# Modulation steps of four tied products, and weights listed in one order and split two k-tiles ahead, in a two-block fp32 network on one core

## The chip, the cores and the metric

The kernel runs on one core of one Trainium2 chip. The metric is the device time of that core in microseconds. TensorE is called PE, VectorE DVE, ScalarE ACT, GpSimd POOL and SyncE SP; SP issues most of the DMAs here, in order.

## The reference

Two blocks in fp32, on 256 tokens of width 2048 with 256 tokens of context. The first block has two layers; each turns a conditioning vector c (and another one for the context) into shift, scale and gate, modulates the normed tokens with them and multiplies with one wide matrix:

```python
for l in range(DEPTH):
    shift, scale, gate = jnp.split(sc @ w_ada[l] + b_ada[l], 3, axis=-1)      # sc = silu(c)
    shift_c, scale_c, gate_c = jnp.split(scc @ w_ada[l] + b_ada[l], 3, axis=-1)
    h = rms(x, norm_w[l]) * (1.0 + scale[:, None]) + shift[:, None]
    hc = rms(xc, norm_w[l]) * (1.0 + scale_c) + shift_c
    qa, ka, va, qb, kb, vb, qc, kc, vc, z = project_stream(h, *weights, rope=(cos, sin))
    ...                                                    # the same for hc, three attentions
    x = x + gate[:, None] * merge_out(o_a, o_b, o_c, z, w_out[l])
```

The second block follows with a token mixer (spatial gating and gated linear attention), a cross attention to a memory, and a convolutional feed-forward:

```python
y = token_mixer(h, w_in, ...);             x = x + rmsnorm(y, post_norm_mix)
y = memory_cross_attention(h, m, ...);     x = x + rmsnorm(y, post_norm_xa)
y = conv_ffn(h, w_up, conv_w, conv_b, w_down);  x = x + rmsnorm(y, post_norm_ffn)
```

## The kernel before

Every large product in fp32 is made of three matmuls of a rounded type. Each operand is split into hi (the value rounded, a copy by ACT, line 376) and lo (the rest, a subtraction by DVE, line 377), and the products are hi by hi, hi by lo and lo by hi. `dense` (lines 420 to 422) has a block of 128 tokens as the stationary operand and 512 weight columns as the moving one; `denseT` (lines 440 to 443) is its transposed form. A k-tile is 128 rows of a weight. `weights` loads two k-tiles with one DMA of 512 KB into one of three tiles `raw`, and splits both into hi and lo tiles, four of each.

In the program each call of `weights` stands at its place, but the framework's scheduler puts the instructions into the order of each engine by priorities and by when buffers come free, so a split may be placed ahead of products that stand before it in the program. The order of each engine is fixed when the kernel is built, and each engine works its own queue in that order.

Stage one (`first_products`) makes the columns of w_in that need the modulation first. The 16 k-tiles of h = modulated x are taken in five parts, `PARTS` = (0,2), (2,2), (4,4), (8,4), (12,4), as first k-tile and count, and called part 0 to part 4 here. A part has three chunks of 512 columns by four blocks of 128 tokens: 72 matmuls named L0firstd in parts 0 and 1, 144 in the others. While part i is multiplied, the modulation of part i+1 is worked out by `ada_pe`: W = 128n columns of shift and W of scale, as 16 steps of one k-tile each. Such a step loads its piece of w_ada (256 KB per DMA) into tiles `raw` of a ring of five and issues two products on the tile `adao`, with the 32-column stationary operand `cstat` (silu of c) and fp32 operands (line 629). The products go to one of four 32-partition places of one PSUM bank, by the k-tile's parity and by shift or scale. After the last step ACT copies the bank (line 634), PE transposes it (line 637), DVE adds the places up, and the next k-tiles of h can be made (transposes `trs`, line 468; hi and lo of h, lines 483 and 484).

The steps are jobs that a planner issues between dense matmuls, one each `self.every` microseconds of its own count of time:

```python
self.every = n * len(chunks) * 2.56 / FIRST
```

In later stages a part of w_ada's work is done by DVE instead (line 668).

Of the kernel before, what the change touches and what calls it, by code (L numbers as in the profile page):

```python
# [10 lines left out]
F32 = mybir.dt.float32  # L11
F32R = mybir.dt.float32r
# [4 lines left out]
UNITS = 50  # L17
FIRST = 20
D = 2048
NKT = D // 128  # L20
# [120 lines left out]


class Weights:


    def __init__(self, ap, name):
        self.ap, self.at, o = ap, {}, 0
# [45 lines left out]
class K:  # L193
# [8 lines left out]
    def __init__(self, ctx, tc, a):  # L202
        self.tc, self.nc, self.a = tc, tc.nc, a
        nc = self.nc
# [8 lines left out]
        self.ps = ctx.enter_context(tc.tile_pool(name="psum", bufs=1, space=bass.MemoryType.PSUM))  # L213
        self.nu = self.alt = 0
        self.vt = self.const.tile([128, NVT], F32, name="vt")
# [173 lines left out]
    def weights(self, w, k0, pieces):  # L389

        nc = self.nc
        raw = self.str.tile([128, 2, 512], F32, name=self.name("raw"), tag="raw", bufs=3)
        n, src = w.block(k0, pieces)
        nc.sync.dma_start(raw[:, :, :n], src)
        out = []
        for j in range(2):
            hi = self.str.tile([128, 512], F32R, name=self.name("hi"), tag="hi", bufs=4)
            lo = self.str.tile([128, 512], F32R, name=self.name("lo"), tag="lo", bufs=4)
            self.split(hi[:, :n], lo[:, :n], raw[:, j, :n])
            out.append((hi, lo))  # L400
        return out

    def dense(self, act, kts, w, pieces, cols, evac, what="d", skip={}):


        nc = self.nc
        n = sum(p[1] for p in pieces)
        ps = {t: self.psum("d", what) for t in cols}
        for i in range(0, len(kts), 2):
# [3 lines left out]
            if ks[-1] == kts[-1]:  # L413
                steps.sort(key=lambda s: cols.index(s[1]))
            for kt, t in steps:
                hi, lo = wt[kt - ks[0]]
# [10 lines left out]
    def denseT(self, act, w, pieces, evac, what="e"):  # L427
# [5 lines left out]
        for k0 in range(0, nk, 2):  # L433
            for j, (hi, lo) in enumerate(self.weights(w, k0, pieces)):
                kt = k0 + j
                xh, xl = act.part(kt, 0), act.part(kt, 1)
                for c in range(nt):
# [140 lines left out]
class Block1(K):  # L578
# [27 lines left out]
    def ada_pe(self, k0, n, cst, done):  # L606
# [6 lines left out]

        def step(kt):
            if kt == 0:
                st[0] = self.psum("o", "ada")
            acc = st[0]
            at = w.offset + k0 * 128 * D * 2 + kt * 128 * 2 * W
            if 2 * W <= 512:
                raw = self.temp("raw", tag="PT", bufs=5)  # L620
                nc.sync.dma_start(raw[:, :2 * W], bass.AP(tensor=w.tensor, offset=at, ap=[[2 * W, 128], [1, 2 * W]]))
                raws = raw[:, :W], raw[:, W:2 * W]
            else:
                raws = [self.temp("raw", tag="PT", bufs=5) for _ in range(2)]
                for b in range(2):
                    nc.sync.dma_start(raws[b], bass.AP(tensor=w.tensor, offset=at + b * W, ap=[[2 * W, 128], [1, W]]))
            for b in range(2):
                q = 64 * (kt % 2) + 32 * b
                nc.tensor.matmul(acc[q:q + 32, :W], lhsT=cst[:, kt, :], rhs=raws[b], start=kt < 2,
                                 stop=kt >= NKT - 2, skip_group_check=True)  # L630

# [12 lines left out]

        return [lambda kt=kt: step(kt) for kt in range(NKT)] + [end]

# [690 lines left out]
    def block1(self):  # L1337
        nc, a, tc = self.nc, self.a, self.tc
        with ExitStack() as es:
# [591 lines left out]
```

## Time and profile before

| | |
|---|---|
| median of 3 runs | 3528.77 us (3526.76 to 3531.81) |
| profiled execution | 3528.03 us, its span 3526.3 us |
| PE busy | 3420.2 us (97%) |
| PE weight loads busy | 2952.3 us (84%) |
| DVE busy | 2299.7 us (65%) |
| ACT busy | 1785.4 us (51%) |
| POOL busy | 321.7 us (9%) |
| DMA | 590.45 MB, mean 167 GB/s |
| mean granted clock of PE | 0.983 |

Busy times are of one profiled execution. Weight loads (PEld) lie beside matmuls. Neighbouring matmuls overlap in the records, so what one costs is read from the distance between starts. A matmul with fp32 operands leaves two records, so "x2" on the tile adao is one product. A clock of 1.00 is 2.4 GHz, of 0.50 1.2 GHz.

### The profile page before, as it was taken

The page shows a single profiled execution, that of the slowest core. Times are in us where ns is not written, and L with a number is a line of the kernel's source. Part 1 is how long each engine was busy: PE and PEld are TensorE (multiplying, and loading weights), DVE is VectorE, ACT ScalarE, POOL GpSimd, SP SyncE. Part 2 cuts the span into 40 slices and gives each one's busy share as a digit, 9 for nine tenths or more (in the row PEclk, how much of TensorE's full clock was granted, in tenths as well). Part 3 has the DMA queues.
Part 4 walks back from the last instruction along what each step waited for, and adds up shares of the span by engine and source line. Part 5 has one row for each costly group of instructions (what it writes and reads, how often), then busy time and mean ns, then how long its engine had stood idle before and what let it go on. Part 6 is the DMA issues. An engine that isn't in the chain of part 4 may idle for free.

```text
span 3526.3 us, 57200 instructions
## 1 busy us (share of the span) xinstructions
PE 3420.2 (97%) x20842; PEld 2952.3 (84%) x20842; DVE 2299.7 (65%) x4939; ACT 1785.4 (51%) x3554; POOL 321.7 (9%) x472
## 2 busy tenths in 40 slices
PE   8999999999999998999999999999999899999998
PEld 3467778888787888887777999999978899999886
DVE  2359889868876475887673555555566766666554
ACT  3235556336525355766463445444555555555544
POOL 0012221103110031111110000000000000000000
PEclk9999999999999999999998999999999999999999
DMA  7745544642465434445544535555655455555555
GB/s 257 228 147 172 140 129 132 210 161 73 145 212 182 156 115 134 144 154 156 161 151 137 186 116 184 184 181 186 197 177 169 147 184 183 183 185 190 194 192 166
DMA packets 226778, 590.45 MB, mean 167 GB/s; under 512 B 39904, under 2 KB 63184, under 8 KB 226496
## 3 DMA queue, kind: packets, MB, share of 16 engines
q1 hardware_dynamic: 221104, 570.41, 50.6%
q0 software_dynamic: 4864, 15.69, 1.4%
q8 instruction: 163, 2.67, 0.3%
q14 instruction: 119, 0.97, 0.1%
q10 hardware_dynamic: 528, 0.71, 0.1%
HBM read 582.48 MB, written 4.24 MB: 166 GB/s over the span
## 4 chain that ended last, share of the span: by engine, by line
PE 54%; issue 12%; DVE 4%; ACT 1%; POOL 1%; DMA 1%; POOLq 0%; SPq 0%; DVEq 0%; ACTq 0%
PE upd L442 5%; PE upd L440 5%; PE upd L443 5%; PE downd L420 2%; PE downd L422 2%; PE downd L421 2%; PE L0outd L420 1%; PE L0outd L422 1%; PE L0outd L421 1%; PE Ss L529 1%; DVE lo L377 1%; PE oo L572 1%; PE vd L420 1%; PE vd L422 1%; PE vd L421 1%
## 5 line engine op out<-in xcount | busy, mean ns | idle before, releaser
L377 DVE TENSOR_TENSOR lo<-raw,hi 128x512 fp32r<-128x512 f32 (+3 forms) x1788 | 1204.5, 679 | 892.0 <-ACT hi L376 886.1
L376 ACT ACTIVATE hi<-raw 128x512 fp32r<-128x512 f32 (+3 forms) x1788 | 1089.7, 614 | 1299.7 <-PE upd L442 190.8
L440 PE MATMUL upd<-hi,hi 128*128 128x256 f32 x1408 | 399.2, 284 | 0.0
L442 PE MATMUL upd<-lo,hi 128*128 128x256 f32 x1408 | 399.1, 283 | 0.0
L443 PE MATMUL upd<-hi,lo 128*128 128x256 f32 x1408 | 398.8, 283 | 0.0
L668 DVE SCALAR_TENSOR_TENSOR scr<-raw,cb 128x512 f32<-128x512 f32 x448 | 297.4, 692 | 26.0 <-DMA raw<-in_w_ada_dram 13.4
L442 PEld LDWEIGHTS upd<-lo,hi 128*128 128x128 f32 x1408 | 270.8, 192 | 0.3 <-DVE lo L484 0.3
L443 PEld LDWEIGHTS upd<-hi,lo 128*128 128x128 f32 x1408 | 270.8, 192 | 0.0
L440 PEld LDWEIGHTS upd<-hi,hi 128*128 128x128 f32 x1408 | 270.7, 192 | 0.0
L355 POOL TENSOR_TENSOR sm<-sm,mhalf 128x2 f32<-128x2 f32 (+4 forms) x116 | 116.7, 1008 | 1401.9 <-DVE sm L354 1396.3
L420 PE MATMUL downd<-hi,hi 128*128 128x512 f32 x352 | 137.7, 391 | 0.0
L422 PE MATMUL downd<-hi,lo 128*128 128x512 f32 x352 | 137.7, 391 | 0.0
L421 PE MATMUL downd<-lo,hi 128*128 128x512 f32 x352 | 137.6, 391 | 0.0
L540 ACT ACTIVATE P<-Ss,sm 128x512 f32<-128x512 f32 (+1 forms) x164 | 99.5, 607 | 67.7 <-DVE sm L536 45.9
L364 ACT ACTIVATE PT<-pTt 128x256 f32<-128x256 f32 x226 | 79.1, 380 | 63.6 <-PE pTt L557 56.2
L420 PE MATMUL L0outd<-hi,hi 128*128 128x512 f32 x256 | 101.2, 395 | 4.3 <-DVE ot L1290 3.0
L443 PE MATMUL L0zd<-hi,lo 128*128 128x512 f32 x256 | 99.7, 392 | 0.9 <-DVE lo L377 0.9
L440 PE MATMUL L0zd<-hi,hi 128*128 128x512 f32 x256 | 100.3, 392 | 0.0
L536 DVE TENSOR_REDUCE sm<-Ss 128x1 f32<-128x512 f32 (+1 forms) x164 | 95.6, 586 | 7.2 <-PE Ss L529 6.3
L442 PE MATMUL L0zd<-lo,hi 128*128 128x512 f32 x256 | 100.1, 391 | 0.0
L421 PE MATMUL L0outd<-lo,hi 128*128 128x512 f32 x256 | 100.1, 391 | 0.0
L422 PE MATMUL L0outd<-hi,lo 128*128 128x512 f32 x256 | 99.3, 391 | 0.2 <-DVE lo L377 0.2
(568 smaller groups left out, 9006.2 us busy)
## 6 DMA issues: line engine op xcount, KB each, us to landing
raw<-in_w_in_dram SPq DMA_DIRECT2D x344, 512.0 KB, 3.5
raw<-in_w_ada_dram SPq DMA_DIRECT2D x384, 256.0 KB, 3.1
raw<-in_ffn_w_up_dram SPq DMA_DIRECT2D x176, 512.0 KB, 3.5
raw<-in_w_out_dram SPq DMA_DIRECT2D x104, 512.0 KB, 4.2
raw<-in_ffn_w_down_dram SPq DMA_DIRECT2D x88, 512.0 KB, 3.9
raw<-in_w_proj_b_dram SPq DMA_DIRECT2D x32, 512.0 KB, 3.7
raw<-in_w_in_dram SPq DMA_DIRECT2D x32, 288.0 KB, 3.3
raw<-in_w_proj_a_dram SPq DMA_DIRECT2D x16, 512.0 KB, 4.3
```

Source lines behind the costliest of these rows:

```text
L355: nc.gpsimd.tensor_tensor(r, ms, self.mhalf[:, :n], op=OP.pow)
L376: self.nc.scalar.activation(hi, src, AF.Copy)
L377: self.nc.vector.tensor_sub(lo, src, hi.bitcast(F32))
L420: nc.tensor.matmul(ps[t][:, a], lhsT=xh, rhs=hi[:, a], start=first, stop=False)
L421: nc.tensor.matmul(ps[t][:, a], lhsT=xh, rhs=lo[:, a], start=False, stop=False)
L422: nc.tensor.matmul(ps[t][:, a], lhsT=xl, rhs=hi[:, a], start=False, stop=last)
L440: nc.tensor.matmul(p, lhsT=hi[:, s], rhs=xh, start=kt == 0 and c % per == 0, stop=False, skip_group_check=True)
L442: nc.tensor.matmul(p, lhsT=hi[:, s], rhs=xl, start=False, stop=False, skip_group_check=True)
L443: nc.tensor.matmul(p, lhsT=lo[:, s], rhs=xh, start=False, stop=kt == nk - 1, skip_group_check=True)
L536: nc.vector.tensor_reduce(nm[:, 0:1], S[:, :nk], op=OP.max, axis=AX.X, negate=True)
L540: nc.scalar.activation(P[:, :nk], S[:, :nk], AF.Exp, bias=nm[:, 0:1], accum_out=nm[:, 1:2])
L668: nc.vector.scalar_tensor_tensor(self.temp("scr"), raw, 1.0, st[s], op0=OP.mult, op1=OP.mult, accum_out=st["p"][:, s, k, q:q + 1])
```

## The change

A step of `ada_pe` now covers two k-tiles and issues four products, one for each of the four places, in the reverse of the order of their loads; the first three of these are tied in TensorE's order to the instruction traced before them (`keep_in_program_order`). The ring has eight tiles in place of five (the three more are taken from another tag). A part has 8 steps and an end in place of 16 and an end, and `FIRST` goes from 20 to 11. At the start a step is issued after every second load of x. The second half of the change is a list of all weights in the order of their use, `order()`. `weights` takes finished splits from a queue `whole`; `run_ahead` loads and splits the next k-tile of the list while the queue holds fewer than two, whatever product it belongs to. It is called twice in each pair of k-tiles of `dense`, and once a k-tile in `denseT`. The numbers of raw, hi and lo buffers stay the same.

```diff
-FIRST = 20
+FIRST = 11
...
+def order():
+    out = []
+    def use(name, pieces, k0=0, n=None):
+        out.extend((name, k, pieces) for k in range(k0, k0 + (n or CHUNKS[name][0] // 128), 2))
...
     def weights(self, w, k0, pieces):
-        nc = self.nc
-        raw = self.str.tile([128, 2, 512], F32, name=self.name("raw"), tag="raw", bufs=3)
-        n, src = w.block(k0, pieces)
-        nc.sync.dma_start(raw[:, :, :n], src)
-        out = []
-        for j in range(2):
-            hi = self.str.tile([128, 512], F32R, name=self.name("hi"), tag="hi", bufs=4)
-            lo = self.str.tile([128, 512], F32R, name=self.name("lo"), tag="lo", bufs=4)
-            self.split(hi[:, :n], lo[:, :n], raw[:, j, :n])
-            out.append((hi, lo))
-        return out
+        assert self.order[self.taken] == (w.name, k0, pieces), (self.order[self.taken], w.name, k0, pieces)
+        self.taken += 1
+        while len(self.whole) < 2:
+            self.run_ahead()
+        return [self.whole.pop(0) for _ in range(2)]
+
+    def load(self):
+        if self.order_at < len(self.order):
+            name, k0, pieces = self.order[self.order_at]
+            self.order_at += 1
+            raw = self.str.tile([128, 2, 512], F32, name=self.name("raw"), tag="raw", bufs=3)
+            n, src = self.w(name).block(k0, pieces)
+            self.nc.sync.dma_start(raw[:, :, :n], src)
+            self.loaded += [raw[:, j, :n] for j in range(2)]
+
+    def run_ahead(self):
+        if not self.loaded:
+            self.load()
+        if self.loaded and len(self.whole) < 2:
+            raw = self.loaded.pop(0)
+            n = raw.shape[-1]
+            hi, lo = (self.str.tile([128, 512], F32R, name=self.name(x), tag=x, bufs=4) for x in ("hi", "lo"))
+            self.split(hi[:, :n], lo[:, :n], raw)
+            self.whole.append((hi, lo))
...
-            for kt, t in steps:
+            for s, (kt, t) in enumerate(steps):
+                if s % -(-len(steps) // 2) == 0:
+                    self.run_ahead()
...
                 kt = k0 + j
+                self.run_ahead()
...
-        def step(kt):
-            if kt == 0:
+        def tile():
+            self.ada_at = (self.ada_at + 1) % 8
+            return self.temp("raw", tag="P", bufs=3) if 4 <= self.ada_at < 7 else self.temp("raw", tag="PT", bufs=5)
+
+        def step(kt0):
+            if kt0 == 0:
                 st[0] = self.psum("o", "ada")
             acc = st[0]
...
-            for b in range(2):
+            for kt, b in reversed(raws):
                 q = 64 * (kt % 2) + 32 * b
-                nc.tensor.matmul(acc[q:q + 32, :W], lhsT=cst[:, kt, :], rhs=raws[b], start=kt < 2,
-                                 stop=kt >= NKT - 2, skip_group_check=True)
+                m = nc.tensor.matmul(acc[q:q + 32, :W], lhsT=cst[:, kt, :], rhs=raws[kt, b], start=kt < 2,
+                                     stop=kt >= NKT - 2, skip_group_check=True)
+                if (kt, b) != (kt0 + 1, 1):
+                    self.tc.keep_in_program_order(m)
...
-        return [lambda kt=kt: step(kt) for kt in range(NKT)] + [end]
+        return [lambda kt=kt: step(kt) for kt in range(0, NKT, 2)] + [end]
...
                 nc.sync.dma_start(x, src)
-                first[i]()
+                if i % 2:
+                    first[i // 2]()
```

Lines move with the change: 629 becomes 698, 420 to 422 become 481 to 483, 376 and 377 become 420 and 421, 668 becomes 739, 902 becomes 973, and 729 and 732 become 800 and 803.

How the order of instructions changes is seen at two places. The first is on PE in stage one, where part 1 is multiplied and part 2's modulation is worked out (numbers behind a name tell its copies apart). Before:

```order
L629 MATMUL adao_579<-raw_608,cstat_130 32x512
L420 MATMUL L0firstd_565<-hi_568,hi_524 128x512
L421 MATMUL L0firstd_565<-lo_569,hi_524 128x512
L422 MATMUL L0firstd_565<-hi_568,lo_525 128x512
L629 MATMUL adao_579<-raw_616,cstat_130 32x512
L629 MATMUL adao_579<-raw_617,cstat_130 32x512
L420 MATMUL L0firstd_565<-hi_572,hi_537 128x512
L421 MATMUL L0firstd_565<-lo_573,hi_537 128x512
L422 MATMUL L0firstd_565<-hi_572,lo_538 128x512
L420 MATMUL L0firstd_647<-hi_653,hi_524 128x512
L629 MATMUL adao_579<-raw_625,cstat_130 32x512
L421 MATMUL L0firstd_647<-lo_654,hi_524 128x512
```

With the change, at the start of the same part:

```order
L481 MATMUL L0firstd_572<-hi_494,hi_524 128x512
L482 MATMUL L0firstd_572<-lo_495,hi_524 128x512
L698 MATMUL adao_585<-raw_592,cstat_130 32x512
L698 MATMUL adao_585<-raw_590,cstat_130 32x512
L698 MATMUL adao_585<-raw_588,cstat_130 32x512
L698 MATMUL adao_585<-raw_586,cstat_130 32x512
L481 MATMUL L0firstd_573<-hi_494,hi_524 128x512
L483 MATMUL L0firstd_572<-hi_494,lo_525 128x512
L481 MATMUL L0firstd_572<-hi_546,hi_537 128x512
L698 MATMUL adao_585<-raw_604,cstat_130 32x512
L698 MATMUL adao_585<-raw_602,cstat_130 32x512
L698 MATMUL adao_585<-raw_600,cstat_130 32x512
```

The modulation's products stood alone or in pairs between dense matmuls; now four stand in a row each time. PE's order of the changed kernel has 24 such groups of W = 512 (one spot has two groups in a row) and, behind the first L0firstd, 8 of W = 256; between the transposes ahead of the first L0firstd none is left.

The second place is on DVE in the product L0cq, late in the first layer, where lo of the weight is made beside the normalizing (lines 729, 732 and 902) and the other share of the modulation (line 668). Before:

```order
L902 TENSOR_TENSOR b_1262_4935<-b_1262_4935,sm_5000 128x512
L729 TENSOR_TENSOR rt_5054<-b_1261_4933,rSqb_1870 128x384
L732 TENSOR_TENSOR ro_5053<-b_1261_4933,rCqb_1869 128x384
L729 TENSOR_TENSOR rt_5058<-b_1261_4933,rSkb_1877 128x128
L732 TENSOR_TENSOR ro_5053<-b_1261_4933,rCkb_1876 128x128
L668 SCALAR_TENSOR_TENSOR scr_5064,adaP_4975<-raw_1309_5062,cb_4976 128x512
L668 SCALAR_TENSOR_TENSOR scr_5066,adaP_4975<-raw_1309_5062,cb_4978 128x512
L668 SCALAR_TENSOR_TENSOR scr_5070,adaP_4975<-raw_1312_5068,cb_4976 128x512
L668 SCALAR_TENSOR_TENSOR scr_5072,adaP_4975<-raw_1312_5068,cb_4978 128x512
L902 TENSOR_TENSOR b_1263_4937<-b_1263_4937,sm_5011 128x512
L377 TENSOR_TENSOR lo_5097<-raw_5094,hi_5096 128x512
L377 TENSOR_TENSOR lo_5101<-raw_5094,hi_5100 128x512
```

With the change, at the same place:

```order
L421 TENSOR_TENSOR lo_5049<-raw_5046,hi_5048 128x512
L973 TENSOR_TENSOR b_1266_4943<-b_1266_4943,sm_4975 128x512
L973 TENSOR_TENSOR b_1267_4945<-b_1267_4945,sm_5006 128x512
L800 TENSOR_TENSOR rt_5060<-b_1266_4943,rSqb_1880 128x384
L803 TENSOR_TENSOR ro_5059<-b_1266_4943,rCqb_1879 128x384
L800 TENSOR_TENSOR rt_5064<-b_1266_4943,rSkb_1887 128x128
L803 TENSOR_TENSOR ro_5059<-b_1266_4943,rCkb_1886 128x128
L739 SCALAR_TENSOR_TENSOR scr_5070,adaP_4981<-raw_1312_5068,cb_4982 128x512
L739 SCALAR_TENSOR_TENSOR scr_5072,adaP_4981<-raw_1312_5068,cb_4984 128x512
L739 SCALAR_TENSOR_TENSOR scr_5076,adaP_4981<-raw_1315_5074,cb_4982 128x512
L739 SCALAR_TENSOR_TENSOR scr_5078,adaP_4981<-raw_1315_5074,cb_4984 128x512
L973 TENSOR_TENSOR b_1268_4947<-b_1268_4947,sm_5017 128x512
```

The 117th lo of the program, lo_5097 before and lo_5049 after, stood behind the four steps of line 668 and the product of line 902 and now stands ahead of them; the 118th, lo_5101 before, stands right behind the last of these rows, as it did.

## Rows read from the trace of the kernel before

**Rows 1.** The page's busy time of each engine, its share of the span, and instructions.
```profile
PE 3420.2 (97%) x20842; PEld 2952.3 (84%) x20842; DVE 2299.7 (65%) x4939; ACT 1785.4 (51%) x3554; POOL 321.7 (9%) x472
```

**Rows 2.** Timeline, PE's first dense product and ACT ahead of it: start, duration.
```profile
33.51 0.61 ACT L483 ACTIVATE hi<-h 128x512 fp32r<-128x512 f32 x1
...
36.10 0.48 PE L420 MATMUL L0firstd<-hi,hi 128*128 128x512 f32 x1
```

**Rows 3.** Stretches: length; PE, PEld, DVE, ACT, POOL busy (instructions); PE clock, DMA share, GB/s.
```profile
60.00:114.00 54.00, 52.72 (x180) 19.78 (x178) 19.01 (x41) 10.32 (x21) 0.00 (x0) 1.00 0.63 196
114.00:168.00 54.00, 54.00 (x221) 30.16 (x223) 23.14 (x43) 15.22 (x28) 0.00 (x0) 1.00 0.75 251
3350.00:3400.00 50.00, 50.00 (x220) 41.17 (x220) 26.19 (x40) 24.64 (x41) 0.00 (x0) 1.00 0.59 192
```

**Rows 4.** The same view for the instructions on the tile adao alone.
```profile
36.00:60.00 24.00, 8.22 (x54) 1.87 (x52) 0.38 (x1) 1.00 0.70 222
60.00:212.00 152.00, 60.89 (x192) 8.22 (x192) 1.80 (x3) 1.00 0.69 226
```

**Rows 5.** Timeline of PE: one product alone, four together, a pair with W = 256.
```profile
99.79 0.40 PE L422 MATMUL L0firstd<-hi,lo 128*128 128x512 f32 x1
100.12 1.04 PE L629 MATMUL adao<-raw,cstat 128*32 128x512 f32 x2
...
101.43 0.39 PE L421 MATMUL L0firstd<-lo,hi 128*128 128x512 f32 x1
...
167.52 0.39 PE L422 MATMUL L0firstd<-hi,lo 128*128 128x512 f32 x1
167.84 1.06 PE L629 MATMUL adao<-raw,cstat 128*32 128x512 f32 x8
...
169.17 0.39 PE L421 MATMUL L0firstd<-lo,hi 128*128 128x512 f32 x1
...
56.00 0.40 PE L422 MATMUL L0firstd<-hi,lo 128*128 128x512 f32 x1
56.33 0.63 PE L629 MATMUL adao<-raw,cstat 128*32 128x256 f32 x4
...
57.22 0.39 PE L421 MATMUL L0firstd<-lo,hi 128*128 128x512 f32 x1
```

**Rows 6.** Timeline of PE at the border between part 1 and part 2.
```profile
109.33 0.66 PE L637 MATMUL adat<-ident,ada 128*128 128x128 f32 x4 [0.69 <-ACT ada L634]
...
111.57 0.55 PE L468 MATMUL trs<-ident,x 128*128 128x128 f32 x3 [0.60 <-DVE h L478]
```

**Rows 7.** A stretch at the start, columns as in the third group.
```profile
20.00:30.00 10.00, 8.70 (x38) 2.52 (x35) 0.62 (x4) 5.08 (x16) 1.09 (x2) 0.50 1.05 391
```

**Rows 8.** DMA issues (median us to landing), SP's issues, and what SP waited for.
```profile
raw<-in_w_ada_dram SPq DMA_DIRECT2D x131, 256.0 KB, 3.4
...
121.09 0.81 SPq L626 DMA_DIRECT2D raw<-in_w_ada_dram  x2
...
SPq L626 <- PE adao L629: 67.0, 41, 3.9
```

**Rows 9.** What PE waited for over the whole span: us, times, longest.
```profile
PE L1qbd L420 <- ACT hi L376: 5.1, 1, 5.1
...
PE L0cqd L421 <- DVE lo L377: 3.9, 2, 3.2
```

**Rows 10.** Timeline of PE after its longest wait in L0cq, and that stretch.
```profile
529.57 0.50 PE L421 MATMUL L0cqd<-lo,hi 128*128 128x512 f32 x1 [3.16 <-DVE lo L377]
...
530.83 0.63 PE L420 MATMUL L0cqd<-hi,hi 128*128 128x512 f32 x1
531.26 0.63 PE L421 MATMUL L0cqd<-lo,hi 128*128 128x512 f32 x1
...
530.00:533.50 3.50, 3.50 (x11) 2.69 (x10) 3.50 (x11) 0.00 (x0) 0.00 (x0) 0.54 0.78 249
```

**Rows 11.** Table loads of ACT: busy time, mean ns of one.
```profile
L1493 ACT ACT_TABLE_LOAD x3 | 3.8, 1283 | 0.1
```

More of the change, by code (lines that the diff above doesn't have):

```diff
@@ L140, in packed_ada @@
     return np.concatenate(out)
+def order():
+    out = []
+    def use(name, pieces, k0=0, n=None):
+        out.extend((name, k, pieces) for k in range(k0, k0 + (n or CHUNKS[name][0] // 128), 2))
+    A = [[(256 * i, 256), (512 + 256 * i, 256)] for i in range(2)]
+    ckv = [[(3584, 288)], [(3872, 288)]]
+    for k0, n in PARTS:
+        for p in [[(1024, 512)]] + A:
+            use("w_in0", p, k0, n)
+    for p in [[(2560, 512)], [(1536, 384), (2304, 128)], _Z[0], [(1920, 384), (2432, 128)], [(3072, 512)], *ckv,
+              _Z[3], _Z[1], _Z[2]]:
+        use("w_in0", p)
+    for l in range(2):
+        if l:
+            for p in [[(2816, 256)], [(1024, 512)], *A, [(2304, 512)], *ckv, [(1536, 384)], [(1920, 384)],
+                      [(3072, 512)], _Z[3], _Z[2]]:
+                use("w_in1", p)
+        for j in range(3):
+            use(f"w_qb{l}", [(384 * j, 384)])
+            use(f"w_kvb{l}", [(512 * j, 512)])
+            if l and j < 2:
+                use("w_in1", _Z[j])
+        for j in range(4):
+            for _ in range(2 if not l and j == 3 else 1):
+                use(f"w_out{l}", [(512 * j, 512)])
+    for p in CHUNKS["w_in_2"][1][:3] + _N512(4, 4096):
+        use("w_in_2", p)
+    for c in (2048, 3072, 2560, 3584, 0, 512, *range(6144, 8192, 512)):
+        use("w_in_2", [(c, 512)])
+    for n in range(4):
+        use("w_in_2", [(8208 + 512 * n, 512)])
+        use("w_in_2", [(10256 + 512 * n, 512)])
+        use("w_proj_a_2", [(512 * n, 512)])
+        use("w_proj_b_2", [(512 * n, 512)])
+    for n in ("w_out_2", "xa_wk_2", "xa_wq_2", "xa_wv_2", "xa_wo_2", "ffn_w_up_2", "ffn_w_down_2"):
+        for p in CHUNKS[n][1]:
+            use(n, p)
+    return out
 class Weights:
     def __init__(self, ap, name):
-        self.ap, self.at, o = ap, {}, 0
+        self.name, self.ap, self.at, o = name, ap, {}, 0
         rows, chunks = CHUNKS[name]
@@ L213, in __init__ @@
         self.ps = ctx.enter_context(tc.tile_pool(name="psum", bufs=1, space=bass.MemoryType.PSUM))
-        self.nu = self.alt = 0
+        self.nu = self.alt = self.ada_at = 0
+        self.order, self.loaded, self.whole, self.taken, self.order_at = order(), [], [], 0, 0
         self.vt = self.const.tile([128, NVT], F32, name="vt")
@@ L612, in ada_pe @@
         st = {}
-        def step(kt):
-            if kt == 0:
+        def tile():
[3 more added lines that the diff above has]
+            if kt0 == 0:
                 st[0] = self.psum("o", "ada")
             acc = st[0]
[L618 to L624, printed above, removed]
+            raws = {}
+            for kt in (kt0, kt0 + 1):
+                at = w.offset + k0 * 128 * D * 2 + kt * 128 * 2 * W
+                if 2 * W <= 512:
+                    raw = tile()
+                    nc.sync.dma_start(raw[:, :2 * W], bass.AP(tensor=w.tensor, offset=at, ap=[[2 * W, 128], [1, 2 * W]]))
+                    raws[kt, 0], raws[kt, 1] = raw[:, :W], raw[:, W:2 * W]
+                    continue
                 for b in range(2):
-                    nc.sync.dma_start(raws[b], bass.AP(tensor=w.tensor, offset=at + b * W, ap=[[2 * W, 128], [1, W]]))
-            for b in range(2):
+                    raws[kt, b] = tile()
+                    nc.sync.dma_start(raws[kt, b], bass.AP(tensor=w.tensor, offset=at + b * W,
+                                                           ap=[[2 * W, 128], [1, W]]))
+            for kt, b in reversed(raws):
                 q = 64 * (kt % 2) + 32 * b
-                nc.tensor.matmul(acc[q:q + 32, :W], lhsT=cst[:, kt, :], rhs=raws[b], start=kt < 2,
-                                 stop=kt >= NKT - 2, skip_group_check=True)
+                m = nc.tensor.matmul(acc[q:q + 32, :W], lhsT=cst[:, kt, :], rhs=raws[kt, b], start=kt < 2,
+                                     stop=kt >= NKT - 2, skip_group_check=True)
+                if (kt, b) != (kt0 + 1, 1):
+                    self.tc.keep_in_program_order(m)
         def end():
```

## The prediction, made before the changed kernel ran

> **What bounds the kernel now.** The page's busy times come first: PE is busy 97% of the span [rows 1]. So a change is worth what it takes out of PE's own row, and work that goes away on another engine is worth nothing. The stretches come next, because both edits to the modulation lie in stage one, from the first L0firstd product at 36.10 us [rows 2] to the last at about 255. In the stretches 60–114 and 114–168 PE is busy 52.72 and 54.00 of 54 us, with 0.63 and 0.75 of the DMA share and a clock of 1.00 [rows 3]. PE bounds stage one, and the transfers have room. The same stretches for the tile adao alone show whose busy time that is: 60.89 of 152 us from 60 to 212 belong to the modulation's products, and 8.22 us more from 36 to 60 [rows 4]. That is the place to look, since a dense 128x512 product costs 50.00/220 = 0.227 us [rows 3].
>
> **What a stop for the modulation costs.** PE's timeline tells it by the starts, not by the durations, since matmuls overlap. A lone product (two records, x2) at 100.12 stands between a dense product at 99.79 and the second one after it at 101.43: 1.64 us, where two dense pitches would be 0.45. The one stop with four products (x8) at 167.84 takes 169.17 − 167.52 = 1.65 us [rows 5]. So a stop costs 1.64 − 0.45 = 1.19 us whether one or four products stand in it: the products of four different 32-partition places run side by side, 1.04 us for one and 1.06 for four. With W = 256 a pair at 56.33 costs 57.22 − 56.00 − 0.45 = 0.76 us [rows 5].
> Now the number of stops. 60.89 us at about 1.05 each are 58 stops of W = 512 [rows 4, 5], for 192 records, which is 96 products: 1.66 products in a stop. 8.22/0.63 = 13 stops of W = 256 lie behind the first dense product.
>
> **The change part by part.**
> *Tying.* The order of the changed kernel has every group as four in a row: 24 groups of W = 512 and 8 of W = 256 behind the first dense product; the first part's steps before 30 us stay bound by the DMA (391 GB/s, share 1.05 [rows 7]) and are costed at nothing. Stops saved: 58 − 24 = 34, times 1.19 = 40.5 us; 13 − 8 = 5, times 0.76 = 3.8 us.
> On the cost of four together the Trainium skill speaks against the row. Its page "TensorE: Matmul & The Clock Gate", section "Measured speedup vs the span model", gives three column tiles side by side a speedup of 2.38, not 3. As an estimate from that page a stop would take 1.26 times a lone one, 0.27 us more, and 24 of them would give 6.5 us back; the trace does not agree, with 1.06 for four against 1.04 for one.
> *Some stops were cover.* At the border of part one PE waits 0.69 us for ACT before the transposes at 109.33, and 0.60 for h before those at 111.57, with three of part 3's products in between that fill the rest [rows 6]. With the stops gone from there such waits are bare: four stops near 107–114 had partly cost nothing. I take 2 us off (0 to 4.8, which is 4 x 1.19).
> *Start.* Before, three W = 256 pairs stand among the transposes ahead of the first dense product at 36.10; in the new order none does. ACT's hi of h starts at 33.51 and takes 0.61 [rows 2], so the first dense product could start at about 34.2: 1.9 us (0 to 1.9). PE runs at a clock of 0.50 in 20–30 [rows 7] and is still at it when the transposes begin, and when it has less to do there that stretch may end later: 1 us against it (0 to 3.5, as long as the stretch of half clock at 530 [rows 10]).
> *Transfers of tied groups.* A group needs four tiles, and the ring has eight, so the loads for a group start when the group two before it is done. While part one's 72 dense products run, the new order has 16 to 27 of them between such groups, which with the group between is 16 x 0.227 + 1.19 = 4.8 us to 7.3 us. Needed are two issues of 0.81 us for two each, and 3.4 us to landing [rows 8]: 5.0 us. In the parts of 144 dense products it is 6 to 8 us. So the stretch of part one sits at the edge; per byte too, since 16 k-tiles of w_ada (8.4 MB) and three loads of w_in (1.6 MB) have to come in 72 x 0.227 + 8 x 1.19 = 25.9 us, 385 GB/s, where the best stretch had 391 [rows 7]. If transfers go there at the 251 GB/s of 114–168 [rows 3], 10 MB take 40 us and PE waits 14; if all fits, 0. Nearer to the landing times, at 1 to 2 us for each of five or six groups, I take 8 us (0 to 15). What waits with PE's group is all dense work behind it, as PE's queue is in order.
> *Splits ahead.* The rows of PE's waits that name hi or lo of a weight come to 26 waits and 23 us, of which L1qbd's 5.1 for ACT and L0cqd's 3.9 for DVE are the largest [rows 9]. The scheduler had already taken splits across borders, within four buffers that the change leaves as they are. Where lo was late on DVE, the order moves it: the lo that PE waited 3.16 us for at 529.57 [rows 10] was behind four L668 steps and one L902 and is now ahead of them. Its sister lo is not moved, so the wait does not go whole. Where ACT's hi was late (5.1 us) the order is as before, behind the same work. I take 4 us (0 to 10; a loss is held off by the order, which has 241 lo earlier, 44 later).
> *Tables.* The order of ACT has two more table loads, 1.283 us each [rows 11], in the stage of L1493 where ACT is busiest: 2 us against it (0 to 2.6).
> *Unchanged:* the instructions on all engines are otherwise the same set, and DVE's side steps of w_ada in later stages stay paced as they were; PE at 97% covers moves on other engines.
>
> **Sum,** against the profiled 3528.0 us: −40.5 − 3.8 + 2 − 1.9 + 1 + 8 − 4 + 2 = −37.2, so 3490.8. The profiled execution is 0.7 under the median, so a median of 3491.5.
>
> **The rivals.**
> *The transfers become the bound of stage one.* The stretch of part one waits 14 us, and two later parts, 8.4 + 3.1 = 11.5 MB each in 144 x 0.227 + 9.5 = 42.2 us (273 GB/s), take 45.9 at 251 GB/s, 3.7 more each: 21 in place of 8, so 3504. For it: no stretch with dense products went beyond 251 GB/s. Against it: SP, which issues them, waited 67 us of the 108 from 60 to 168 for PE to release tiles [rows 8], so these stretches show what was asked for and not what can be had. Chance 0.13.
> *Splits and transfers both go well.* No DMA wait, and 15 of the 23 us of split waits go: 8 + 11 less, so 3472. For it: lo moves earlier at most late places; against it: the ACT ones stand. Chance 0.14.
> *Four together are dearer than the one row of four says.* If a group cost as much as two pairs one after the other, 1.05 more each, 24 groups give 25 us back: 3516. Only one stop of four stands in the trace, but pairs and threes cost the same 1.65. Chance 0.03; the page's rule cited above would be its mild form.
> *The other side: waits that drop the clock.* At 529.57, after a wait of 3.16 us, dense products of 128x512 go from 530.83 to 531.26, 0.43 us apart, at the 1.2 GHz level instead of 2.4, in a stretch of some 3.5 us at a clock of 0.54 [rows 10]. If each tied group waits as long for its transfers, and 8 products after it run at 0.43 instead of 0.227, a group costs 3.2 + 1.6 = 4.8 us more; all 24 cost 115 in place of 8, so 3598. It decides the sign from 45/4.8, more than nine groups, on. The row that speaks against it is SP's wait above. The Trainium skill, page "TensorE: Matmul & The Clock Gate", section "Loop structure matters more than you think", calls a DMA wait ahead of each group of matmuls the bad loop, since PE goes cold in it; the trace agrees on the effect, at 530, and no row here shows it in stage one. Chance 0.04.
> *Nothing gained:* the stops cost PE nothing, because something else paces stage one. PE's 54.00 of 54 us speaks against it: 0.02.
>
> **How the numbers follow.** Forecast 0.64, from 3480 to 3503; it and the rivals make 1. The measurement tells a difference of about 0.2%, 7 us (its runs spread over 5). Faster: 0.64 + 0.13 + 0.14 + 0.03 = 0.94; same 0.02; slower 0.04. The range goes to the better case, −57 with the remaining bounds, and to the DMA case: 3468 to 3508. Outside are about a third of those two, the dearer groups, the clock and nothing gained: 0.18.
>
> **What would show it.** Right: dense products and groups of four in stage one at 1.65 us from the one before to the second after; adao's busy time near 24 x 1.06 + 8 x 0.63 = 30 us where it was 69; the last L0firstd near 219 instead of 255; waits of PE on w_ada of some 8 us in part one; L0cqd's wait under 2 us, L1qbd's 5.1 as before. Wrong: waits on w_ada over 20 us, or windows in stage one with a clock under 1.00; a group over 1.3 us; or a late stage that moves by more than 10 us, as the splits are the only thing that changed there.

## The result, and the profile after

The changed kernel takes 3488.55 us (median of 4 runs, 3481.28 to 3491.26), the kernel before 3527.77 beside it: a ratio of 0.989, 95% interval 0.9864 to 0.9915. The profiled execution took 3488.5 us (its span 3486.4). The forecast was 3491, in a range from 3468 to 3508.

On the page, PE's busy time falls by 59.7 us against [rows 1], more than the time does; DVE's and ACT's hardly move:

```profile
PE 3360.5 (96%) x20842; PEld 2937.7 (84%) x20842; DVE 2296.0 (66%) x4939; ACT 1786.5 (51%) x3556; POOL 318.3 (9%) x472
```

The stretches of stage one (columns as in [rows 3]) show three things: the start, with the DMA as busy as before; a stretch of part 1 in which PE is busy only 26.41 of 30 us; and a stretch at a clock of 0.66 behind it, which [rows 3] did not have.

```profile
20.00:30.00 10.00, 5.42 (x34) 1.81 (x34) 0.62 (x4) 4.26 (x13) 1.09 (x2) 1.00 1.05 396
60.00:90.00 30.00, 26.41 (x142) 14.97 (x138) 13.26 (x26) 4.92 (x9) 0.00 (x0) 1.00 0.89 299
90.00:100.00 10.00, 8.56 (x33) 3.81 (x34) 4.06 (x8) 2.86 (x6) 0.00 (x0) 0.66 0.61 201
100.00:140.00 40.00, 39.65 (x200) 27.15 (x198) 20.78 (x39) 13.44 (x25) 0.00 (x0) 1.00 0.89 307
```

The clock of 1.00 in the first of these rows is not borne out by PE's own rows. Four products of W = 256 at 29.97 take 1.08 us and four at 36.09 take 0.64, as a pair at full clock took 0.63 [rows 5]: in this stretch PE ran at 1.2 GHz, as in [rows 7]. The trace has no record of the clock ahead of 32.8 us, and the view gives 1.00 where there is none. From the timeline of the start:

```profile
29.97 1.08 PE L698 MATMUL adao<-raw,cstat 128*32 128x256 f32 x8
...
34.76 0.61 ACT L545 ACTIVATE hi<-h 128x512 fp32r<-128x512 f32 x1
...
35.42 0.50 PE L481 MATMUL L0firstd<-hi,hi 128*128 128x512 f32 x1
...
36.09 0.64 PE L698 MATMUL adao<-raw,cstat 128*32 128x256 f32 x8
```

For the tile adao alone, where [rows 4] had 8.22 and 60.89:

```profile
36.00:60.00 24.00, 6.03 (x72) 1.42 (x72) 0.38 (x1) 1.00 0.77 259
60.00:180.00 120.00, 26.18 (x188) 3.82 (x184) 1.79 (x3) 0.97 0.82 274
```

32.2 us in place of 69.1: the modulation's stops are gone as counted. PE's timeline has the price of one stop, as in [rows 5]: from 110.09, ahead of a group of four, to 111.74, the second dense product behind it, 1.65 us. The only place with two groups in a row takes 142.41 − 139.90 = 2.51.

```profile
110.09 0.39 PE L483 MATMUL L0firstd<-hi,lo 128*128 128x512 f32 x1
110.41 1.06 PE L698 MATMUL adao<-raw,cstat 128*32 128x512 f32 x8
...
111.74 0.39 PE L482 MATMUL L0firstd<-lo,hi 128*128 128x512 f32 x1
...
139.90 0.39 PE L483 MATMUL L0firstd<-hi,lo 128*128 128x512 f32 x1
140.22 1.93 PE L698 MATMUL adao<-raw,cstat 128*32 128x512 f32 x16
...
142.41 0.39 PE L482 MATMUL L0firstd<-lo,hi 128*128 128x512 f32 x1
```

What PE waited for between 36 and 232 us (us, times, longest):

```profile
PE trs L530 <- DVE h L540: 4.3, 1, 4.3
PE adao L698 <- DMA raw<-in_w_ada_dram: 2.0, 3, 1.2
...
```

The 4.3 us are at the border between part 1 and part 2, the place of [rows 6]. From the timeline of all engines there:

```profile
86.54 0.60 PE L708 MATMUL adat<-ident,ada 128*128 128x128 f32 x4
...
87.51 1.15 ACT L420 ACTIVATE hi<-raw 128x512 fp32r<-128x512 f32 x2 [1.21 <-DVE a L1403]
88.18 0.69 DVE L421 TENSOR_TENSOR lo<-raw,hi 128x512 fp32r<-128x512 f32 x1 [0.75 <-ACT hi L420]
88.78 0.25 DVE L712 TENSOR_REDUCE adaT<-adat 128x8 f32<-128x16 f32 x2
...
88.98 0.17 DVE L664 SCALAR_TENSOR_TENSOR adaT<-adaT,vt 128x8 f32<-128x8 f32 x1
89.07 0.68 DVE L421 TENSOR_TENSOR lo<-raw,hi 128x512 fp32r<-128x512 f32 x1
89.67 0.16 DVE L665 TENSOR_TENSOR adaT<-adaT,vt 128x8 f32<-128x8 f32 x1
89.75 0.16 DVE L666 TENSOR_TENSOR adaT<-adaT,vt 128x8 f32<-128x8 f32 x1
89.83 0.69 DVE L421 TENSOR_TENSOR lo<-raw,hi 128x512 fp32r<-128x512 f32 x1
90.43 1.65 DVE L540 SCALAR_TENSOR_TENSOR h<-trs,adaT,rb 128x256 f32<-128x256 f32 x4
...
91.44 0.45 PE L530 MATMUL trs<-ident,x 128*128 128x128 f32 x1 [4.30 <-DVE h L540]
```

The chain from the modulation to the next h runs over adat on PE (86.54), adaT (lines 712, 664 to 666) and h (line 540) on DVE. DVE's queue has three lo (line 421) of weights among these steps, at 88.18, 89.07 and 89.83; the first waits 0.75 us for ACT's hi. In [rows 6] the same chain took PE from 109.33 to 111.57; here it takes it from 86.54 to 91.44.

Where the 40 us lie is read by lining up the same products in both traces. The first L0firstd starts 0.7 us earlier. Stage one's last product starts 36.25 us earlier (265.39 to 229.14 by the trace's own clock, whose zero lies some 10 us ahead of the span's; 218.7 on the span's). The last product of the program starts 39.92 earlier. So 3.7 us came behind stage one.

### The profile page after: what moved, and what is told of

Its sections match the earlier page's. It is cut to its first block, busy times and chain, and to the rows that moved or that the text cites. A ratio compares the mean times of both kernels' runs of the same rounds, so it can differ in the third digit from the quotient of the medians.

```text
span 3486.4 us, 57207 instructions
## 1 busy us (share of the span) xinstructions
PE 3360.5 (96%) x20842; PEld 2937.7 (84%) x20842; DVE 2296.0 (66%) x4939; ACT 1786.5 (51%) x3556; POOL 318.3 (9%) x472
```

## The experiments

Ratios are to the kernel before as measured beside each run (3525.73 to 3526.96 us); differences from the change are to its 3488.55, and for the last three runs to its second measure. "Stage one ends" gives the start of the last L0firstd on the trace's clock, 265.39 before and 229.14 with the change.

**The modulation alone.** The kernel before with the new `ada_pe`, FIRST and start; `weights` as before.

Against the kernel before, with the rest of `ada_pe` as in the change's diff:

```diff
-FIRST = 20
+FIRST = 11
...
-        def step(kt):
+        def step(kt0):
...
+            for kt, b in reversed(raws):
...
-                first[i]()
+                if i % 2:
+                    first[i // 2]()
```

> The kernel before with the modulation half of the change alone: steps of two k-tiles, eight tiles in the ring, products in reverse order and tied, FIRST 11, loads of x and w_ada two by two at the start. Weights are loaded and split as before. By the theory of stops (each stop for modulation costs PE 1.19 us with W = 512 and 0.76 with W = 256, and the splits are worth next to nothing) it takes nearly all of the gain: its order has 22 and 7 stops behind the first dense product, and part 2's modulation ends at the 120th dense product and not at the 144th, so the bare wait of 4.3 us at that border goes too: 3488 (3483 to 3495). The rival, that the list of weights with its splits ahead brings a third of the gain (13 us), expects 3501.

Measured: 3499.49 (3495.18 to 3503.84), ratio 0.9928 (0.9912 to 0.9944). Stage one ends at 235.54. It has most of the gain, but 11 us less than the change: outside the first expectation's range and near the rival's 3501. The waits of tied groups for w_ada which the prediction had feared are here, and with them a lower clock; the second row is the longest of five waits, 8.3 us in all, and the third a stretch:

```profile
66.15 1.55 PE L636 MATMUL adao<-raw,cstat 128*32 128x512 f32 x8 [2.19 <-DMA raw<-in_w_ada_dram]
...
86.00 1.94 PE L636 MATMUL adao<-raw,cstat 128*32 128x512 f32 x8 [3.13 <-DMA raw<-in_w_ada_dram]
...
60.00:95.00 35.00, 27.65 (x125) 16.13 (x122) 10.25 (x21) 2.88 (x7) 0.00 (x0) 0.80 0.80 270
```

The 4.3-us wait at the border is not there: the modulation ends at the 120th product, and 24 products are left to cover its chain. Three lo stand among the chain's steps on DVE here too:

```profile
89.97 1.28 DVE L377 TENSOR_TENSOR lo<-raw,hi 128x512 fp32r<-128x512 f32 x2
...
91.46 0.69 DVE L377 TENSOR_TENSOR lo<-raw,hi 128x512 fp32r<-128x512 f32 x1
```

But its order has groups so early that the transfers don't follow. Stage one is 6.4 us longer than in the change, and the remainder 3.7 us longer.

**The splits alone.**

Against the change, with `ada_pe` as in the kernel before:

```diff
-FIRST = 11
+FIRST = 20
...
-        def step(kt0):
+        def step(kt):
...
-                if i % 2:
-                    first[i // 2]()
+                first[i]()
```

> The changed kernel with the modulation as before (steps of one k-tile, five tiles, FIRST 20), so that only the list of weights and the splits two k-tiles ahead are left of the change. By the theory of stops, with 56 and 16 stops in its order where before had 57 and 13, it is 3520 to 3528, with lo's wait in L0cq at about 2 us where it was 3.9. The rival, that splits ahead bring a third, expects 3515 or less.

Measured: 3520.44 (3516.99 to 3529.13), ratio 0.9989 (0.9978 to 1.0): some 5 us, at the edge of what can be told. Stage one ends 1.1 us later than before; the gain lies behind it. L0cq's wait is 2.2 us. At the border no lo stands in the chain, and PE waits 0.6 us for h. The theory of stops holds; the splits don't bring a third of the gain.

**The products of a step in the order of their loads.**

```diff
-            for kt, b in reversed(raws):
+            for kt, b in raws:
...
-                if (kt, b) != (kt0 + 1, 1):
+                if (kt, b) != (kt0, 0):
```

> The changed kernel with the four products of a step traced in the order of their loads instead of the reverse; loads, ring, ties, FIRST and splits are unchanged. Its order has 51 stops of W = 512 and 9 of W = 256, where the change has 23 and 8: the first product need not wait for the last load, and dense products get between. By the theory of stops: 28 x 1.19 + 0.76 = 34 us more, 3522 (3513 to 3528). The rival, that the longer steps, the ring and the pace bring the gain and the number of stops doesn't matter, expects 3488.

Measured: 3515.54 (3512.44 to 3519.29), ratio 0.9973 (0.9963 to 0.9984). Stage one ends at 258.45, 29.3 us later than in the change. Two thirds of the gain hang on the direction of one loop: with the last load's product first, the other three are ready and follow it at once; with the first load's product first, dense products slip in between. adao's busy time:

```profile
36.00:262.00 226.00, 62.16 (x256) 9.39 (x256) 2.18 (x4) 1.00 0.60 196
```

The expected 34 is off by things that the fewer stops had cost elsewhere: here the border wait is 1.9 and not 4.3, the waits for w_ada 0.4 and not 2.0, and there is no half clock at the border: 34 − 2.4 − 1.6 − 3.4 = 26.6, 2.7 short of what was measured. That the ties themselves do nothing can be read without a run: the changed kernel built without `keep_in_program_order` is the same program, instruction for instruction, in the order of all five engines.

**Steps of one k-tile, ring of eight.**

```diff
-FIRST = 11
+FIRST = 20
...
-            for kt in (kt0, kt0 + 1):
+            for kt in (kt0,):
...
-                if (kt, b) != (kt0 + 1, 1):
+                if b != 1:
...
-        return [lambda kt=kt: step(kt) for kt in range(0, NKT, 2)] + [end]
+        return [lambda kt=kt: step(kt) for kt in range(NKT)] + [end]
...
-                if i % 2:
-                    first[i // 2]()
+                first[i]()
```

> The changed kernel with steps of one k-tile (two products in a row), FIRST 20 and a w_ada load after every load of x, but with the ring of eight and all else as in the change. Its order has 47 stops of W = 512 and 15 of W = 256. By the theory of stops: 24 x 1.19 + 7 x 0.76 = 34 us more than the change, 3522 (3513 to 3528). If the ring and the splits brought the gain: 3488 to 3495.

Measured: 3513.24 (3507.47 to 3516.39), ratio 0.9967 (0.9954 to 0.998). Stage one ends 25.8 us later than in the change, with the border wait at 1.7 us, no wait for w_ada and no half clock at the border: 34 − 2.6 − 2.0 − 3.4 = 26.0. adao's busy time:

```profile
36.00:262.00 226.00, 59.24 (x252) 8.94 (x252) 2.18 (x4) 1.00 0.61 198
```

So the price of a stop holds in two kernels that differ in other ways, to within 3 us in some 30 stops.

**Run-ahead that stops at the end of a product.**

```diff
-        if not self.loaded:
+        if not self.loaded and (now or at < len(self.order) and self.first[at] == self.first[self.taken - 1]):
             self.load()
```

(`first` is the place in the list where an entry's product begins; `weights` calls with `now`.)

> The changed kernel whose run-ahead stops at the end of a product: the list, the calls and the ties stay, but a k-tile of the next product is loaded and split in the program only when that product asks for it. Its order puts part 2's modulation earlier, to the 120th dense product, as in the run with the modulation half alone, where PE waited 8.3 us for w_ada in stage one. Theory now: (a) stage one ends some 6 us later than in the change, at 235 instead of 229 for the last L0firstd, with 6 to 9 us of waits for w_ada; (b) behind stage one the crossing is worth the 4 us that the change gained there over the kernel before. Together 3497 to 3501. The rival, that the crossing does nothing since the scheduler moves splits across borders anyway, expects 3489 in all, or at least no difference behind stage one.

Measured: 3486.27 (3484.95 to 3493.18), ratio 0.9888 (0.9873 to 0.9903). Part (a) came nearly as expected: stage one ends at 233.10, 4.0 us later than in the change, with these waits on w_ada:

```profile
PE adao L703 <- DMA raw<-in_w_ada_dram: 9.0, 5, 3.4
```

Part (b) fell: the remainder is not longer without the crossing but 7.2 us shorter than in the change, so crossing product borders is not what helps behind stage one (by one profiled execution of each).

**Modulation issued a part earlier.** The first with a = 2 and FIRST 13, the second with a = 3 and FIRST 14.

```diff
-            if i + 1 < len(PARTS):
-                for f in steps(i + 1):
-                    self.push(f)
+            todo = (steps(1) if i == 0 else rest)
+            rest = steps(i + 2) if i + 2 < len(PARTS) else []
+            for f in todo + rest[:a]:
+                self.push(f)
+            rest = rest[a:]
```

> The changed kernel with two of the eight steps of each further part's modulation issued one part earlier, and FIRST 13. Its order ends part 2's modulation at the 136th dense product where the change has it at the 144th, the end of the part. By the theory that the change's 4.3-us wait for h at that border and the half clock behind it (6.8 us, of which about half is lost) come from modulation that ends with the part: the wait halves and the clock stays at 1.00, 3482 to 3486. By the rival, that PE then waits for w_ada instead, since the loads of that stretch come in at no more than they do now: 3488 or more.

> As the run with two steps earlier, with three steps and FIRST 14; part 2's modulation ends at the 120th dense product, with groups as near as 7 to 10 dense products to one another. By the border theory the wait for h goes whole: 3480 to 3483. By the rival, waits for w_ada of 4 to 8 us in the stretch before take its place, as in the run with the modulation half alone: 3488 to 3492.

Measured: 3492.51 (3489.4 to 3495.32), ratio 0.9902 (0.9887 to 0.9917), and 3493.79 (3493.14 to 3495.8), ratio 0.9907 (0.989 to 0.9923). The border theory alone is wrong: the wait for h goes in both, and waits for w_ada take its place, first with two steps, then with three:

```profile
PE adao L698 <- DMA raw<-in_w_ada_dram: 5.8, 7, 1.1
```

```profile
PE adao L698 <- DMA raw<-in_w_ada_dram: 8.1, 6, 3.4
```

**A ring of five.**

```diff
-            self.ada_at = (self.ada_at + 1) % 8
-            return self.temp("raw", tag="P", bufs=3) if 4 <= self.ada_at < 7 else self.temp("raw", tag="PT", bufs=5)
+            return self.temp("raw", tag="PT", bufs=5)
```

> The changed kernel with five tiles in the ring for w_ada instead of eight. The order still has the groups of four, 22 and 8 stops, but 15 to 17 dense products apart, and part 3's and 4's modulation end behind their borders. A group's loads can't start before the group ahead of it is done (one tile alone is free): two issues of 0.81 us and 3.4 us to landing are 5.0 us against 16 x 0.227 = 3.6 us of dense work, so PE should wait 1.4 us a group, some 20 to 30 us in all and at the borders more: 3508 to 3525. If the ring is not what lets the ties pay: 3488 to 3495.

Measured: 3525.2 (3519.23 to 3530.52), ratio 0.9995 (0.9986 to 1.0004): at the upper end of the expectation. Nothing is left of the gain, with 22 stops of W = 512 in place of 57. What 35 fewer stops saved, PE waits away, and after the longest waits the clock stands at 0.50 for 22 us:

```profile
PE adao L697 <- DMA raw<-in_w_ada_dram: 32.3, 21, 4.8
...
93.13 1.93 PE L697 MATMUL adao<-raw,cstat 128*32 128x512 f32 x8 [4.36 <-DMA raw<-in_w_ada_dram]
...
92.00:114.00 22.00, 8.40 (x37) 2.43 (x41) 3.02 (x11) 3.07 (x7) 0.73 (x1) 0.50 0.65 206
```

In this kernel four in a row pays only with tiles for the next four. This is the rival of the other side, waits that drop the clock, in a kernel where it does decide.

**The change again,** with no edit.

> The changed kernel itself once more, as the measure for the three runs beside it: 3488.5 (3483 to 3492). If its 4 earlier runs were a lucky draw: above 3492.

Measured: 3489.81 (3487.13 to 3490.34), ratio 0.9891 (0.9874 to 0.9908). Its border wait is 3.5 us, its waits for w_ada 3.0, and the half clock behind them some 7 us: a group that takes 1.06 us at full clock takes 1.94.

```profile
92.79 0.45 PE L530 MATMUL trs<-ident,x 128*128 128x128 f32 x1 [3.46 <-DVE h L540]
93.16 1.94 PE L698 MATMUL adao<-raw,cstat 128*32 128x512 f32 x8
```

**A ring of eleven.**

```diff
-            self.ada_at = (self.ada_at + 1) % 8
+            self.ada_at = (self.ada_at + 1) % 11
+            if self.ada_at < 3:
+                return self.B("raw", tag="raw2", bufs=3)
```

> The changed kernel with eleven tiles in the ring for w_ada instead of eight. In the change SP waited 18.2 us of the 42 from 50 to 92 for PE to release such tiles. If the ring sets the transfers of that stretch, the 2 us of waits for w_ada go and little else, since its order still ends part 2's modulation with the part and three lo of the next product's weight still stand on DVE ahead of that part's chain: 3484 to 3488. If the transfers are at their bound (359 GB/s in 80 to 90 us): 3488 or more.

Measured: 3481.97 (3478.27 to 3485.04), ratio 0.987 (0.9854 to 0.9886), 7.8 us under the change beside it, and better than either theory said. Stage one ends at 223.70, 6.5 us earlier than in that run. The waits for w_ada are gone (3.0 us), and so is the half clock (7 us, of which half is lost: 3.5). The wait for h at the border is still there and just as long, but the clock behind it stays at 1.00:

```profile
90.08 0.30 PE L530 MATMUL trs<-ident,x 128*128 128x128 f32 x1 [3.46 <-DVE h L540]
...
85.00:105.00 20.00, 16.46 (x91) 9.55 (x88) 11.55 (x26) 9.65 (x19) 0.00 (x0) 1.00 0.94 329
```

Whether the ring kept the clock up or chance did is not shown: one execution of each was profiled.

**No loads of w_ada in stage one but the first eight.**

```diff
+            kept = self.__dict__.setdefault('kept', [])
...
+                if len(kept) == 8:
+                    for b in range(2):
+                        raws[kt, b] = kept[(2 * kt + b) % 8][:, :W]
+                    continue
...
+                    kept.append(raw)
...
```

> The changed kernel without the loads of w_ada in stage one, but for the first eight; all later products of the modulation reuse those tiles, so its modulation is wrong. It prices what the transfers still cost. Its order has the same 24 groups of W = 512, and the 8 stops of W = 256 ahead of the first dense product. By the theory that the stops are what the modulation costs PE: 24 x 1.19 us stay, 8 x 0.76 = 6 us move into the wait at the start, the 9.2-us wait for w_ada there goes in part, and waits, border and half clock of some 8 us go: 3466 to 3476. If transfers cost nothing any more in the change: 3482.

Measured: 3465.26 (3462.2 to 3470.6), ratio 0.9825 (0.9808 to 0.9841), 24.6 us under the change beside it and just under the first theory's range. Stage one ends at 208.26, 22.0 us earlier. The products of W = 256 stand in two rows ahead of the first dense product, two groups and then these six; it starts 5.1 us earlier, though PE still waits 9.5 us for the first loads:

```profile
27.82 2.80 PE L704 MATMUL adao<-raw,cstat 128*32 128x256 f32 x48
30.54 0.50 PE L481 MATMUL L0firstd<-hi,hi 128*128 128x512 f32 x1
```

6 us for these stops, 5 for the start, 3.0 of waits, 3.5 of border and 3.5 of half clock are 21 of the 22. So transfers, and what hangs on them (the order too, which ends part 2's modulation at the 123rd product here), still cost some 15 us in the change.

**Three edits together:** run-ahead inside a product, a ring of eleven, two steps earlier with FIRST 13 (diffs above).

> Three edits together on the changed kernel: run-ahead stops at the end of a product, the ring has eleven tiles, and two steps of each further part's modulation are issued one part earlier with FIRST 13. By the theory that the change loses some 8 us at the end of part 1 (three splits of the next product ahead of the modulation's chain on DVE) and that such a version without more tiles only traded it for waits on w_ada (9.0 us): both go, 3478 to 3484. By the rival that the stretch is bound by the rate of the transfers: waits on w_ada of 5 us or more stay, 3485 to 3490.

Measured: 3479.76 (3473.76 to 3485.88), ratio 0.9864 (0.9845 to 0.9884), the lowest of the kernels that load all of w_ada, and not to be told from the ring of eleven alone. Stage one ends at 229.37, no earlier than in the change, with these waits:

```profile
PE adao L705 <- DMA raw<-in_w_ada_dram: 3.0, 2, 2.6
```

Its gain lies behind stage one, so the theory for which it was built did not bring it.

## Why the prediction was right, step by step

**Stops, −44.3: right, in number and price.** By the trace, 22 stops of four at 1.2 us, one of eight at 2.05 and eight of W = 256 at 0.78 cost 34.7 us; 57 stops at 1.19 and 13 at 0.76 cost 77.7 before: −43.0. The kernels with 51 and 47 stops bear the price out. The speedup of 2.38 for three column tiles side by side that the Trainium skill gives, page "TensorE: Matmul & The Clock Gate", section "Measured speedup vs the span model", does not show here as a dearer stop: four take 1.06 us where one took 1.04 [rows 5].

**Stops that were cover, +2: the place right, the reason wrong.** The border costs 3.0 us more than before (4.3 against 0.69 + 0.60), and another 3.4 through the half clock behind it. Nothing of the prediction had said that splits would stand on DVE among the steps of the modulation's chain, and it had no term for a lower clock in stage one. That the three lo lengthen the wait is read from DVE's queue (3 x 0.69 + 0.75 = 2.8 us of the 3.0) and was not tried by moving them alone. They are not enough for it: the modulation alone has three lo in its chain too, and no wait for h, since its modulation ends 24 products ahead of the border. With two steps earlier it ends 8 products ahead, no lo stands in the chain, and that wait is gone too.

**Start, −1.9 + 1: −0.7.** The first dense product starts right behind ACT's hi of h, as was said (hi ends at 35.37, the product starts at 35.42). But this hi starts at 34.76 and not at 33.51: the last four products of part 0's modulation stand behind an instruction of PE that waits 2.1 us for POOL, start at 29.97 only, and the chain to h runs 1.25 us later. The fear for the clock did not come true in this execution, where the half clock ends at 32.8, ahead of the first dense product; in the second measure of the change it ends at 37.7, 2 us behind it.

**Transfers of tied groups, +8: mis-sized at 2.0 us of waits,** 3.0 in the second measure. The order spaces the groups as far as their loads need. The worst case went by 251 GB/s, said to be the most in any stretch with dense products; that was a mean over 54 us, and the kernel before has 293 in a stretch in which PE is busy throughout:

```profile
60.00:70.00 10.00, 10.00 (x39) 4.72 (x37) 6.10 (x15) 4.96 (x10) 0.00 (x0) 1.00 0.85 293
```

The change has 307 from 100 to 140. The step was right as a mechanism: in the modulation-alone kernel it is 8.3 us, with a ring of five 32.3. Whether the transfers also cost clock in the change is open: with the ring of eleven stage one is 6.5 us shorter, 3.0 by waits and 3.5 by a half clock that did not come in that execution.

With these, −43.0 + 3.0 + 3.4 − 0.7 + 2.0 = −35.3 for stage one, measured −36.25, so 1 us is not accounted for. The prediction's terms for it come to −35.2. That these sums agree so well is luck in part: the transfers were put 6 us too high, the border and the half clock behind it 4.4 us too low, and the stops 1.3 us too good.

**Splits, −4: the number near, the step wrong.** The waits for splits sum to 25.1 us over the whole span, where the same number, 26, came to 24.5 (not to the 23 of the prediction). What L0cq and L1qb gained on DVE, vs and mb lost on ACT, where mb had 0.7. Before, beside L0cqd's row in [rows 9]:

```profile
PE L1qbd L421 <- DVE lo L377: 3.9, 3, 2.4
...
PE vsd L420 <- ACT hi L376: 1.4, 2, 1.0
```

With the change:

```profile
PE L1qbd L481 <- ACT hi L420: 5.1, 1, 5.1
PE vsd L481 <- ACT hi L420: 4.2, 3, 2.6
...
PE mbd L502 <- ACT hi L420: 2.2, 2, 1.2
PE L0cqd L482 <- DVE lo L421: 2.2, 1, 2.2
...
PE L1qbd L482 <- DVE lo L421: 1.7, 3, 1.1
```

All waits behind stage one went from 76.8 to 83.8 us. Where the kernels differ is the clock: the half clock there (from windows of 10 us, twice the share missing to 1.00) came to 101 us before and 105 with the modulation alone, and to 71 to 94, with a mean of 85, in the twelve runs that have the list, at waits of 77 to 84. At half clock about half the time is lost: 16 x 0.5 = 8 us. From the first L0vb to the last product those two kernels take 3255.2 us each; the twelve 3240.9 to 3254.5, with a mean of 3249.0. If waits and half of the half clock are taken off, all fourteen lie between 3124 and 3133. So the list goes with 6 us in the mean, in kernels with less time at 1.2 GHz. That the clock is the cause is not shown: the change's own two profiled executions have 71 and 88 us at half clock, waits of 84 and 78, and the same remainder to 0.3 us. The stretches lie at other places from run to run, no stretch was removed by itself, and the two kernels whose run-ahead stops at the product's end have the shortest remainder, one of them by only 0.6 us.

In stage one the list did what the prediction had no term for. With the modulation alone, and with run-ahead inside a product, part 2's modulation ends at the 120th product, and PE waits 8.3 and 9.0 us for w_ada; with the crossing it ends at the 144th, and stage one is 6.4 and 4.0 us shorter.

**Tables, +2.** The loads are there, three each at the two lines where there were two; they lie in the stage where vs waits for ACT, and were not tried alone:

```profile
L1586 ACT ACT_TABLE_LOAD x3 | 3.8, 1283 | 0.1
L1591 ACT ACT_TABLE_LOAD x3 | 3.8, 1283 | 0.1
```

**The rivals.** The DMA as the bound: not in the change; with eight tiles, waits for w_ada are what stops an earlier modulation (two and three steps earlier). Splits and transfers both going well: the transfers nearly did, the splits did not, and 3472 was not reached. The drop of the clock by waits: 6.8 us of it in the change, 27 with a ring of five, where it and the waits take all the gain. Four together dearer: no. Nothing gained: no.

**What would show it.** The stop of 1.65 us, adao's 32.2 us against 30, the last L0firstd at 218.7 against 219 and L1qbd's 5.1 came as named. L0cqd's wait is 2.2 us and not under 2, and the waits for w_ada are 2.0 us and not 8. One sign of being wrong came too: a window in stage one with a clock under 1.00.

## What to carry to other kernels

Where side-by-side products cost PE the same singly and together, count stops, not products, and look in the built order for what decides whether they stand together: here the direction in which four products are traced, not the call that was meant to tie them. A group takes its gain only if the buffers hold the next group while this one is worked; look then at the engine that issues its loads, and at how long it waits for tiles. For each chain that crosses a stage border on an in-order engine, look at what other work stands among its steps, and at how much work is left to cover it. And where a clock column says 1.00, hold it against the time that like products take.

## What the runs showed of the hardware that was not expected

A stop of four costs 1.65 − 0.45 = 1.2 us, and the one place with eight in a row 2.51 − 0.45 = 2.06: the second four adds 0.86. So, as an estimate from that place, some 0.34 us of each stop is for going from one kind of product to the other and back, and 0.86 for the products themselves. The run without loads agrees for W = 256: six groups in a row take 2.80 us and one takes 0.64, so each further group adds 0.43, and of a stop of 0.78 some 0.35 is left.

A wait does not by itself lower the clock. In the second measure of the change PE waited 3.46 us at the border and ran at 1.2 GHz behind it; in the ring of eleven it waited 3.46 us at the same place and stayed at 2.4 GHz; with a ring of five three waits of 4.36 to 4.83 us followed one another, and the clock stood at 0.50 for 22 us.
